# Seven products for the last six input tiles of the second down projection, in a two-layer hybrid model kernel

## The chip, the cores and the metric

The kernel runs on one core of one Trainium2 chip. The metric is the device time of one execution in microseconds (us), as the median of several runs. Before the change it is 2143.97 us, the median of 3 runs that lie between 2143.37 and 2144.52 us.

## What is computed

The reference is a model of two layers on one sequence of T = 1024 tokens with D = 1024 channels, all in float32. Each layer is a mixer followed by a feed-forward block with a short causal convolution, both added to a running sum `h`; a last norm scales the result. The change lies in the feed-forward blocks and in that last norm:

```python
def conv_ffn(hn, w_up, conv_w, conv_b, w_down):
    up = causal_dwconv(hn @ w_up, conv_w) + conv_b
    gate, val = jnp.split(up, 2, axis=-1)
    return (jax.nn.silu(gate) * val) @ w_down
...
        h = h + conv_ffn(rms_norm(h, norm_ffn[layer]), ffn_w_up[layer], ...)
    return rms_norm(h, norm_final)
```

The hidden width is 2816, which is 22 tiles of 128 channels. So the down projection of a layer has 22 input tiles and 8 output tiles.

## The kernel before

Everything is kept with channels on the 128 partitions and tokens along the free axis. `H[0..7]` are the eight channel tiles of the running sum, each 128x1024. A float32 product is made of three TensorE matmuls (`mm3`, L316): each operand is split into a high part and a low part (hi is a rounded copy, lo the difference), and hi·hi, hi·lo and lo·hi are summed in PSUM.

**Seven products.** Most projections are not done tile by tile but two output tiles at a time by a Strassen scheme: the weight block of two output tiles and the token blocks are combined so that seven products stand for eight. `load_pair` (L285) loads four weight pieces and makes seven weight operands from them on ScalarE (ACT) and VectorE (DVE). `pair_product` (L766) runs one product: for each of its `kk` input tiles one `mm3` over 512 columns. There are seven moving operands, o = 0 to 6, of which four are token blocks themselves or a first difference that is stored already split ("whole" ones), and three must be loaded and split again.

**The feed-forward block** (`ffn`, L823). For p = 0 to 21 the up projection of one pair of gate and value tiles runs as seven products; `gate` and `hidden` (L934, L939) do the convolution and the product, and `store_parts` (L863) writes the operands of the down projection to DRAM: whole ones as hi and lo to `p_dram` (L880), others as they are to `s_dram` (L881). All of these DMAs, the two loads that the second half of the tiles needs (L894, L895), the weights (L292) and the operand loads are issued on one queue, SyncE's (SP).

The down projection then runs in sets c of input tiles: sets 0 and 1 have 8 tiles each (two halves of 4, so kk = 4), for t = 0 to 3 pairs of output tiles and o = 0 to 6. While the last pair (t = 3) of a set runs, `load_set` (L908) fills each operand's place for the next set as soon as a product has read it. A whole operand is 8 DMAs of 256 KB (L914) straight into its place. For the others, each piece is first loaded into one of eight half buffers of "room" (L917, L922), that is, `R` and three 128x1024 tiles of the pool `tp`, and then ACT writes hi (L924) and DVE lo (L925) into the place.

The two layers differ. Layer 0 (`third` is true) has a set 2 for the last 6 input tiles, kk = 3, also by seven products. Its operands lie in other places than those of the set before, so that a place freed by product o takes operand (o + 4) % 7: operands 0 to 3 come four products after their place is free, the others eleven. Layer 1 has only sets 0 and 1, with every operand in its own old place, seven products later. Its last 6 input tiles are stored as plain split tiles (L870, two DMAs of 512 KB a tile), loaded by `load_parts`, and multiplied in `final` without the scheme: 8 output tiles x 6 input tiles x `mm3`.

**The end** (`final`, L1036, with `part`, L516). Three stretches of tokens follow one another, of 512, 256 and 256 columns, here called s0, s1 and s2. Each goes through output tiles m = 0 to 7: 18 matmuls, then DVE adds PSUM to `H[m]` (L553), ACT squares it (L407), DVE sums the squares (L411). The weights are loaded and split once (`load_kept`, L276) and kept in the memory `s1`. The norm of s0 goes beside TensorE, through DVE, GpSimd (POOL) and DRAM (`norm_beside`, L424). That of s1 goes through TensorE: `norm_tok` (L456) sums over partitions by matmuls with ones (L480), DVE and POOL make the factor (L470 to L472), and `norm_row` (L482) spreads it by matmuls (L489). `norm_tok` of s1 is put after m = 2 of s2, `norm_row` after m = 4. The scaling of s0 and s1 (`scale`, L1041) is put beside the tiles of s2, every second tile of s0 on POOL (L1047).

**What sets the order.** TensorE's instructions, and those of all other engines, are not run quite as they are written: a planner in the framework puts each engine's instructions in a fixed list by its own estimate of when each is ready, so a load may stand in the queue earlier than the code has it. On the chip each engine and each queue then works through its list in order, and an instruction that waits holds up all behind it.

Of the kernel before, what the change touches and what calls it, by code (L numbers as in the profile page):

```python
# [13 lines left out]
F32 = mybir.dt.float32  # L14
# [89 lines left out]
class Block:  # L104
    def __init__(self, ctx, tc, I, out, stop=None):
# [34 lines left out]
        pad(self.perm, 104, "pad2")  # L140
        self.nhalo = 0
# [45 lines left out]
    def quarter_order(self):  # L187
# [10 lines left out]
        for layer in range(2):  # L198
# [11 lines left out]
            if layer == 0:  # L210
                o += [(("ffn_v0", t), 7) for t in range(4)]
# [611 lines left out]
    def ffn(self, layer, gain):  # L823
        nc, I = self.nc, self.I
        V, A = nc.vector, nc.scalar
        third = gain is not None
        sets = 3 if third else 2
        y_dram = self.tc.dram_tile([NPAIR, P, T], F32, name=f"yf_dram{layer}")
        s_dram = self.tc.dram_tile([sets, 5, 4, P, HALF], F32, name=f"sf_dram{layer}")

        p_dram = self.tc.dram_tile([sets, 4, 4, 2, P, HALF], F32, name=f"pf_dram{layer}")
        if not third:
            l_dram = self.tc.dram_tile([NPAIR - 16, 2, P, T], F32, name=f"lf_dram{layer}")
        depth = lambda c: 4 if c < 2 else 3

        def where(c, o):

            if c == 0 or not third:
                return self.operand(o)
            if c == 1:  # L840
                return self.operand((o + 3) % 7)
            if o < 3:
                i = (20, 14, 26)[o]
                return self.slots1(i, 6).rearrange("p (s n c) -> p n s c", n=2, c=256)
            return self.s2[:, :, 6 * (o - 3):6 * (o - 2), :]
# [15 lines left out]
        room, loads = {}, [0, 0, 0]  # L861

        def store_parts(p, y, hi):  # L863

            hi = hi.bitcast(F32R)
            lo = self.parts.tile([P, T], F32R, tag="lo", name="lo")
            if p >= 16 and not third:
                self.split_half(y, (hi, lo))
                for e, t in enumerate((hi, lo)):
                    nc.sync.dma_start(l_dram[p - 16, e], f32(t))  # L870
                return
# [9 lines left out]
            store = lambda o, r: nc.sync.dma_start(s_dram[c, place[o], k % kk], r)  # L881
# [12 lines left out]
            nc.sync.dma_start(halves(t3), blocks(y_dram[p - kk])[:, :, 1])  # L894
            nc.sync.dma_start(t2, s_dram[c, place[1], k - kk])  # L895
# [9 lines left out]
            else:  # L905
                nc.sync.dma_start(halves(s_dram[c, place[5], k % kk]), v[:, :, 0])

        def load_set(c, o):  # L908
# [7 lines left out]
            if c not in room:  # L916
                ts = [self.R] + [self.t() for _ in range(3)][::-1]  # L917
                room[c] = [t[:, i * HALF:(i + 1) * HALF] for i in range(2) for t in ts]
            for k in range(kk):
                r = room[c][loads[c] % 8]  # L920
                loads[c] += 1
                nc.sync.dma_start(r, s_dram[c, place[o], k])  # L922
                hi, lo = (x[:, :, e + k, :] for e in (0, kk))
                A.copy(hi, halves(r))  # L924
                V.tensor_tensor(lo, halves(r), f32(hi), ALU.subtract)  # L925

        def load_parts(p):
            places = self.place2(p - 16)
            for n in range(2):
                for e in range(2):  # L930
                    nc.sync.dma_start(f32(places[n][e]), l_dram[p - 16, e][:, n * HALF:(n + 1) * HALF])
            return places
# [6 lines left out]
        def hidden(p, tg):  # L939
            tv = conv(NPAIR + p, self.halo[1])  # L940
            V.tensor_tensor(tg, tg, tv, ALU.mult)  # L941
            if (third or p < 16) and p % 8 < depth(p // 8):
# [25 lines left out]
        ys = {}  # L968
        following = {0: {1: (4, 5), **{o: ((o + 4) % 7,) for o in range(2, 7)}},
                     1: {2: (0,), 3: (1, 2), 4: (3,), 5: (4,), 6: (5, 6)}}  # L970
        plain = {0: {1: (0, 1), **{o: (o,) for o in range(2, 7)}}, 1: {}}
        for c in range(sets):
            done = self.down_steps(gain) if c == 2 else {}
            for t in range(4):
                sums, banks = self.pair_added(t), {}
                key = (f"ffn_w{layer}", c, t) if c < 2 else (f"ffn_v{layer}", t)
                for o in range(7):
                    sums(o, self.pair_product(banks, o, self.quarter(key, o), x=where(c, o)))
                    if t == 3 and c < 2:
# [983 lines left out]
```

## Time and profile before

| | us |
|---|---|
| median of 3 runs | 2143.97 |
| the profiled execution's own time | 2145.08 |
| its span, from the first to the last instruction | 2143.2 |
| PE (TensorE matmul) busy | 2127.4 |
| DVE busy | 1722.2 |
| ACT busy | 1077.3 |
| POOL busy | 100.5 |

The profile is of one execution. In its views PE is the matmul side of TensorE and PEld its weight loads; SPq and POOLq are DMA queues; L820 is line 820 of the kernel before. In a table of windows, `(x87)` is the number of recorded instructions that fall into the stretch, PEclk the share of its clock that TensorE was granted, and "DMA share" the mean busy share of the 16 DMA engines. A matmul is shown with its full duration, though the next starts before it ends; its pace is the distance from start to start. A few matmul records are missing.

### The profile page before, as it was taken

To read this page: it belongs to the slowest core of one execution; us is meant where nothing else is said; L and a number is where in the kernel's file an instruction comes from. 1 tells how busy PE (TensorE), PEld (TensorE's weight loads), DVE (VectorE), ACT (ScalarE), POOL (GpSimd) and SP (SyncE) were. 2 spreads that over 40 slices of the span, in tenths; PEclk is the share of its full clock that TensorE was granted. 3 is DMA by queue.
4 is the path that set the end of the run, shared out by engine and by line. 5 is a ranking of instruction groups with operands and counts; after the bars stand their busy time and mean duration, and the time that the engine had idled before them with its cause. 6 is when DMAs were issued, how large, how long until landed. Compare 5 with 4: busy or idle time off the path is not lost.

```text
span 2143.2 us, 29749 instructions
## 1 busy us (share of the span) xinstructions
PE 2127.4 (99%) x10648; PEld 1771.9 (83%) x10648; DVE 1722.2 (80%) x2630; ACT 1077.3 (50%) x1750; POOL 100.5 (5%) x115
## 2 busy tenths in 40 slices
PE   9999999999999999999999999999999999999998
PEld 7878888888888888887888888888888888888887
DVE  7995677776998989988868786768999889878645
ACT  6444423135665555555324576756655555554222
POOL 0102122300000000000000000000000000000002
PEclk9999999999999999999999999999999999999999
DMA  5354433543145435448745212142354445375542
GB/s 188 91 170 126 136 94 94 172 142 118 46 172 178 160 137 179 172 172 289 233 161 172 72 57 80 64 158 65 123 186 163 149 151 177 118 262 183 182 169 85
DMA packets 242021, 313.23 MB, mean 146 GB/s; under 512 B 62432, under 2 KB 129424, under 8 KB 241872
## 3 DMA queue, kind: packets, MB, share of 16 engines
q1 hardware_dynamic: 205632, 304.15, 42.5%
q10 hardware_dynamic: 35088, 6.36, 1.5%
q8 instruction: 84, 1.38, 0.3%
q0 software_dynamic: 1152, 0.81, 0.2%
q14 instruction: 65, 0.53, 0.1%
HBM read 215.79 MB, written 95.45 MB: 145 GB/s over the span
## 4 chain that ended last, share of the span: by engine, by line
PE 63%; issue 30%; DVE 3%; DMA 2%; POOL 1%; SPq 0%; ACT 0%; POOLq 0%; DVEq 0%
PE ps L319 19%; PE ps L320 18%; PE ps L321 18%; PE pc L319 1%; PE pc L321 1%; PE pc L320 1%; DMA s<-pf_dram 1%; DMA t<-sf_dram 0%; DVE wlo L273 0%; DVE l L1416 0%; DVE l L1418 0%; DVE h L1387 0%; PE pc L1551 0%; PE ps L1595 0%; PE pc L1663 0%
## 5 line engine op out<-in xcount | busy, mean ns | idle before, releaser
L319 PE MATMUL ps<-s,whi 128*128 128x512 f32 (+1 forms) x2692 | 1049.1, 391 | 1.5 <-DVE h L820 0.9
L320 PE MATMUL ps<-s,whi 128*128 128x512 f32 (+1 forms) x2692 | 1044.1, 388 | 2.1 <-DVE s L925 1.9
L321 PE MATMUL ps<-s,wlo 128*128 128x512 f32 (+1 forms) x2692 | 1042.7, 388 | 0.6 <-DVE wlo L273 0.6
L272 ACT CAST whi<-raw 128x512 fp32r<-128x512 f32 (+2 forms) x616 | 374.1, 613 | 611.9 <-PE ps L320 471.6
L319 PEld LDWEIGHTS ps<-s,whi 128*128 128x128 f32 x2692 | 505.8, 188 | 107.0 <-ACT whi L272 1.6
L320 PEld LDWEIGHTS ps<-s,whi 128*128 128x128 f32 x2692 | 505.9, 188 | 106.1 <-DVE s L925 4.6
L321 PEld LDWEIGHTS ps<-s,wlo 128*128 128x128 f32 x2692 | 505.6, 188 | 104.5 <-DVE wlo L273 1.4
L273 DVE TENSOR_TENSOR wlo<-raw,whi 128x512 fp32r<-128x512 f32 (+2 forms) x616 | 415.0, 680 | 50.8 <-ACT whi L272 42.3
L852 DVE SCALAR_TENSOR_TENSOR t<-halo,cols,t 128x1024 f32<-128x1024 f32 x176 | 221.6, 1281 | 2.4 <-ACT t L850 1.0
L820 DVE TENSOR_TENSOR h<-ps,h 128x512 f32<-128x512 f32 x140 | 96.3, 689 | 75.7 <-PE ps L321 75.5
L810 DVE TENSOR_TENSOR halo<-ps,kept 128x512 f32<-128x512 f32 (+1 forms) x138 | 91.8, 666 | 71.1 <-PE ps L321 70.5
L850 ACT ACTIVATE t<-halo,cols 128x1024 f32<-128x1024 f32 x88 | 109.5, 1247 | 18.0 <-DVE halo L810 9.0
L805 ACT COPY kept<-ps 128x512 f32<-128x512 f32 (+1 forms) x138 | 77.0, 558 | 11.0 <-PE ps L321 9.6
L472 POOL TENSOR_TENSOR rtok<-rtok,npow 128x4 f32<-128x4 f32 (+1 forms) x10 | 9.9, 990 | 1097.2 <-DVE rtok L471 1097.2
L877 ACT CAST t<-t 128x512 fp32r<-128x512 f32 x68 | 41.2, 621 | 39.1 <-DVE t L941 37.1
L941 DVE TENSOR_TENSOR t<-t 128x1024 f32<-128x1024 f32 x44 | 53.6, 1219 | 0.0
L553 DVE TENSOR_TENSOR h<-ps,h 128x512 f32<-128x512 f32 (+1 forms) x48 | 28.6, 599 | 30.6 <-PE ps L321 30.5
L882 DVE TENSOR_TENSOR t<-t 128x512 f32<-128x512 f32 x76 | 52.1, 686 | 0.6 <-DMA sf_dram<-t 0.6
L936 ACT ACTIVATE t<-t 128x1024 f32<-128x1024 f32 x44 | 46.8, 1063 | 10.4 <-DVE t L852 10.3
L407 ACT ACTIVATE t<-h 128x512 f32<-128x512 f32 (+1 forms) x49 | 26.9, 564 | 45.8 <-DVE h L553 43.8
L878 DVE TENSOR_TENSOR lo<-t 128x512 fp32r<-128x512 f32 x68 | 46.7, 686 | 0.0
L294 DVE TENSOR_TENSOR raw<-raw 128x512 f32<-128x512 f32 (+1 forms) x64 | 43.6, 681 | 3.3 <-issue 1.9
(341 smaller groups left out, 2170.7 us busy)
## 6 DMA issues: line engine op xcount, KB each, us to landing
raw<-in_ffn_up_dram SPq DMA_DIRECT2D x176, 256.0 KB, 2.7
s<-pf_dram SPq DMA_DIRECT2D x136, 256.0 KB, 5.2
sf_dram<-t SPq DMA_DIRECT2D x84, 256.0 KB, 2.4
pf_dram<-t SPq DMA_DIRECT2D x68, 256.0 KB, 2.6
pf_dram<-lo SPq DMA_DIRECT2D x68, 256.0 KB, 2.6
t<-sf_dram SPq DMA_DIRECT2D x67, 256.0 KB, 4.8
raw<-in_ffn_w_dram SPq DMA_DIRECT2D x64, 256.0 KB, 3.1
raw<-in_mix_in_dram SPq DMA_DIRECT2D x52, 256.0 KB, 3.0
```

The lines of the kernel that those rows point to most:

```text
L272: self.nc.scalar.copy(hi[:, 0:w], raw[:, 0:w])
L273: eng.tensor_tensor(lo[:, 0:w], raw[:, 0:w], f32(hi[:, 0:w]), ALU.subtract)
L319: mm(ps, whi, xhi, start=start, stop=False)
L320: mm(ps, whi, xlo, start=False, stop=False)
L321: mm(ps, wlo, xhi, start=False, stop=stop)
L805: A.copy(kept[o], ps)
L810: V.tensor_tensor(dst(i, j), v(ps), v(kept[k]), ALU.add)
L820: V.tensor_tensor(h(*to[o]), ps.rearrange("p (h c) -> p h c", c=256), h(*to[o]), ALU.add)
L850: A.activation(t, buf[:, 2:2 + T], AF.Identity, scale=w(0), bias=self.col(f"ffn_cb{layer}", tile_i))
L852: V.scalar_tensor_tensor(t, buf[:, 2 + j:2 + j + T], w(j), t, ALU.mult, ALU.add)
L882: sub = lambda out, a, b: V.tensor_tensor(halves(out), a, b, ALU.subtract)
L941: V.tensor_tensor(tg, tg, tv, ALU.mult)
```

## The change

1. `store_parts` issues the stores and loads of tiles p = 16 to 21 on POOL's queue, no longer SP's, in both layers. Layer 1 stores these tiles as layer 0 does: per tile 5 DMAs of 256 KB (p = 16 to 18, besides `y_dram` on SP) or 9 (p = 19 to 21, two of them loads).
2. `load_set` has no room any more: a piece that must be split is loaded into the place of its low part, ACT copies hi from there, and DVE takes hi off in place. This holds for both layers. It can start only when the place is free.
3. Layer 1 gets a set 2, and rotates its operands in set 1 as layer 0 does. Its set 2 runs the seven products for t = 0 and 1 only, that is, for output tiles 0 to 3. An eighth operand (o = 7) is loaded during it.
4. `final` computes only m = 4 to 7 by the plain product, from four of the set's operands. The weights of these tiles take 8 places. The squares of `H[0..3]` go over 1024 columns (`final_steps`).
5. The norm of s0 goes through TensorE: `norm_tok` after m = 4 of s1, `norm_row` after m = 5; that of s1 likewise in s2. All tiles of s0 and s1 are scaled on DVE, those of s0 beside m = 6 and 7 of s1 and m = 4 and 5 of s2, those of s1 beside m = 6 and 7 of s2.
6. A spare tile of 40 columns in the pool `sm` takes the 320 bytes of a partition that `norm_beside` no longer needs, so that the operand memory `s2` behind it keeps its address.

```diff
+        pad(self.sm, 40, "pad3")
...
-            if layer == 0:
-                o += [(("ffn_v0", t), 7) for t in range(4)]
+            o += [((f"ffn_v{layer}", t), 7) for t in range(2 if layer else 4)]
...
+            i = ((8, 0, 26, 6, 12, 0, 18, 20) if layer else (20, 14, 26, 0, 6, 12, 18))[o]
+            if o < 3 or o == 7:
                 return self.slots1(i, 6).rearrange("p (s n c) -> p n s c", n=2, c=256)
-            return self.s2[:, :, 6 * (o - 3):6 * (o - 2), :]
+            return self.s2[:, :, i:i + 6, :]
...
+            queue = nc.gpsimd if p >= 16 else nc.sync
...
-            if p >= 16 and not third:
-                self.split_half(y, (hi, lo))
-                for e, t in enumerate((hi, lo)):
-                    nc.sync.dma_start(l_dram[p - 16, e], f32(t))
-                return
...
-                    nc.sync.dma_start(p_dram[c, whole[c][o], k % kk, e], f32(t[:, at]))
-            store = lambda o, r: nc.sync.dma_start(s_dram[c, place[o], k % kk], r)
+                    queue.dma_start(p_dram[c, whole[c][o], k % kk, e], f32(t[:, at]))
+            store = lambda o, r: queue.dma_start(s_dram[c, place[o], k % kk], r)
...
-            if c not in room:
-                ts = [self.R] + [self.t() for _ in range(3)][::-1]
-                room[c] = [t[:, i * HALF:(i + 1) * HALF] for i in range(2) for t in ts]
             for k in range(kk):
-                r = room[c][loads[c] % 8]
-                loads[c] += 1
-                nc.sync.dma_start(r, s_dram[c, place[o], k])
                 hi, lo = (x[:, :, e + k, :] for e in (0, kk))
-                A.copy(hi, halves(r))
-                V.tensor_tensor(lo, halves(r), f32(hi), ALU.subtract)
+                if o < 7:
+                    nc.sync.dma_start(f32(lo), halves(s_dram[c, place[o], k]))
+                else:
+                    nc.sync.dma_start(f32(lo), blocks(y_dram[16 + k])[:, :, 1])
+                A.copy(hi, f32(lo))
+                V.tensor_tensor(lo, f32(lo), f32(hi), ALU.subtract)
...
-                     1: {2: (0,), 3: (1, 2), 4: (3,), 5: (4,), 6: (5, 6)}}
-        plain = {0: {1: (0, 1), **{o: (o,) for o in range(2, 7)}}, 1: {}}
+                     1: {1: (1,), 3: (0, 2), 4: (5,), 5: (3,), 6: (4, 6)} if layer
+                     else {2: (0,), 3: (1, 2), 4: (3,), 5: (4,), 6: (5, 6)}}
+        for c in range(3):
+            done = {}
+            if c == 2:
+                done = self.final_steps() if layer else self.down_steps(gain)
+            for t in range(2 if layer and c == 2 else 4):
...
+    def final_steps(self):
+        V, A = self.nc.vector, self.nc.scalar
+        self.acc, self.sq = self.t(), self.t()
+        def square(m):
+            def f():
+                if m == 0:
+                    A.activation(self.acc, self.H[m], AF.Square)
+                    return
+                A.activation(self.sq, self.H[m], AF.Square)
+                V.tensor_tensor(self.acc, self.acc, self.sq, ALU.add)
+            return f
+        self.squares = square
+        return {(1, 1): [square(0)], (1, 3): [square(1)]}
...
+        kept, places = {}, [6, 14, 16, 18, 0, 2, 4, 26]
+        def part(t0, w, room, left):
...
+            for m in range(4, KT):
+                ps = self.pp(both=True)[:, 0:w]
+                for u in range(2):
+                    if (u, m) not in kept:
+                        kept[u, m] = self.load_kept(self.I[name + "ab"[u]][m], places[len(kept)])
+                    hi, lo = kept[u, m]
+                    for kt in range(4 - 2 * u):
+                        c = slice(kt * P, (kt + 1) * P)
+                        xh, xl = (operand(4 * u + kt, e, n, j) for e in range(2))
+                        self.mm3(ps, hi[:, c], lo[:, c], xh, xl, u == 0 and kt == 0, u == 1 and kt == 1)
+                        self.slot()
+                h = self.H[m][:, sl]
+                V.tensor_tensor(h, ps, h, ALU.add)
+                self.square_step(st, m, h, w)
+                for f in left.get(m, ()):
+                    f()
...
-        s0 = part(0, 512, {})
-        self.norm_beside(s0[0], 0)
-        s1 = part(512, 256, {})
-        late = {k: [lambda k=k: scale(*s0, k, R0, nc.gpsimd if k % 2 else V)] for k in range(KT)}
+        late = lambda s, ks, row: [lambda k=k: scale(*s, k, row()) for k in ks]
+        s0 = part(0, 512, more, {4: [self.squares(2)], 5: [self.squares(3)]})
+        s1 = part(512, 256, self.sq[:, 0:HALF],
+                  {4: [lambda: run(self.norm_tok(s0[0]))], 5: [lambda: run(self.norm_row(s0[0], 0))],
+                   6: late(s0, (0, 1), R0), 7: late(s0, (2, 3), R0)})
...
+        s2 = part(768, 256, self.sq[:, HALF:],
+                  {4: late(s0, (4, 5), R0) + [lambda: run(self.norm_tok(s1[0], 256))],
+                   5: late(s0, (6, 7), R0) + [lambda: run(self.norm_row(s1[0], w=256))],
+                   6: late(s1, range(5), R1), 7: late(s1, range(5, 8), R1)})
```

More of the change, by code (lines that the diff above doesn't have):

```diff
@@ L825, in ffn @@
         V, A = nc.vector, nc.scalar
-        third = gain is not None
-        sets = 3 if third else 2
         y_dram = self.tc.dram_tile([NPAIR, P, T], F32, name=f"yf_dram{layer}")
[L829 to L833, printed above, removed]
+        s_dram = self.tc.dram_tile([3, 5, 4, P, HALF], F32, name=f"sf_dram{layer}")
+        p_dram = self.tc.dram_tile([3, 4, 4, 2, P, HALF], F32, name=f"pf_dram{layer}")
         depth = lambda c: 4 if c < 2 else 3
         def where(c, o):
-            if c == 0 or not third:
+            if c == 0:
                 return self.operand(o)
@@ L893, in store_parts @@
             t4 = t3
-            nc.sync.dma_start(halves(t3), blocks(y_dram[p - kk])[:, :, 1])
-            nc.sync.dma_start(t2, s_dram[c, place[1], k - kk])
+            queue.dma_start(halves(t3), blocks(y_dram[p - kk])[:, :, 1])
+            queue.dma_start(t2, s_dram[c, place[1], k - kk])
             store_split(3, v[:, :, 1], first)
@@ L905, in store_parts @@
             else:
-                nc.sync.dma_start(halves(s_dram[c, place[5], k % kk]), v[:, :, 0])
+                queue.dma_start(halves(s_dram[c, place[5], k % kk]), v[:, :, 0])
         def load_set(c, o):
@@ L941, in hidden @@
             V.tensor_tensor(tg, tg, tv, ALU.mult)
-            if (third or p < 16) and p % 8 < depth(p // 8):
+            if p % 8 < depth(p // 8):
                 nc.sync.dma_start(y_dram[p], tg)
@@ L978, in ffn @@
                     sums(o, self.pair_product(banks, o, self.quarter(key, o), x=where(c, o)))
-                    if t == 3 and c < 2:
-                        for q in (following if third else plain)[c].get(o, ()):
+                    if t == 3:
+                        for q in following[c].get(o, ()):
                             load_set(c + 1, q)
-                    if not third and (c, t) == (1, 3) and o in (1, 2):
-                        for p in range(16, 20) if o == 1 else (20, 21):
-                            ys[p] = load_parts(p)
+                    if layer and (c, t, o) == (2, 0, 1):
+                        load_set(2, 7)
                     for f in done.get((t, o), ()):
@@ L988, in ffn @@
                     hidden(NPAIR - 1, gate(NPAIR - 1))
-        if not third:
-            self.final([ys[p] for p in range(16, NPAIR)], f"ffn_d{layer}")
+        if layer:
+            self.final(f"ffn_d{layer}")
+    def final_steps(self):
[11 more added lines that the diff above has]
+        return {(1, 1): [square(0)], (1, 3): [square(1)]}
     def down_steps(self, gain):
@@ L1034, in xplace, with final @@
         return ((0, 1, 2, 5, 3, 4, 6, 7)[k] * 4 + 2 * e) * HALF
-    def final(self, ys, name):
+    def final(self, name):
         nc = self.nc
         V = nc.vector
+        more = self.t()
         def scale(st, sl, k, pr, eng=V, queue=nc.sync):
```

44 lines of the change are left out of this document (15 added, 29 removed).

## The prediction

> **What bounds the kernel now.** I read the page's table of engines first, then a table of windows cut at the borders of the down projections' sets, then the timeline of TensorE at those borders, and last the waits.
>
> ```profile
> span 2143.2 us, 29749 instructions
> PE 2127.4 (99%) x10648; PEld 1771.9 (83%) x10648; DVE 1722.2 (80%) x2630; ACT 1077.3 (50%) x1750; POOL 100.5 (5%) x115
> ```
>
> TensorE is busy for 99% of the span, so time is won by taking matmuls out or by closing the few places where it starves, and lost by new waits of TensorE. The timeline gives the pace and the price of a norm on TensorE: the first plain matmul of s0, the first two of s1, and, from the end of layer 0, three matmuls around `norm_tok` and three around `norm_row` of a 512-column norm.
>
> ```profile
> 2064.92 0.39 PE L319 MATMUL ps<-s,s 128*128 128x512 f32 x1
> ...
> 2097.56 0.28 PE L319 MATMUL ps<-s,s 128*128 128x256 f32 x1
> 2097.68 0.28 PE L320 MATMUL ps<-s,s 128*128 128x256 f32 x1
> ...
> 1208.09 0.40 PE L321 MATMUL ps<-s,wlo 128*128 128x512 f32 x1
> 1208.42 0.65 PE L480 MATMUL pc<-t,ones 128*32 128x128 f32 x16
> 1208.99 0.50 PE L319 MATMUL ps<-s,whi 128*128 128x512 f32 x1
> ...
> 1209.56 0.40 PE L321 MATMUL ps<-s,wlo 128*128 128x512 f32 x1
> 1209.80 1.05 PE L489 MATMUL pc<-ident,rtok 128*128 128x128 f32 x8
> 1210.60 0.47 PE L319 MATMUL ps<-s,whi 128*128 128x512 f32 x1
> ```
>
> s0 has 8 x 6 x 3 = 144 matmuls between 2064.92 and 2097.56: 32.64 / 144 = 0.2267 us for 512 columns. For 256 columns the distance is 0.12 us. So a set of 336 matmuls takes 76.16 us at this pace, and layer 0's set 2 (252) takes 57.12 us. The windows are, in order: layer 0's set 0, the stretch in it with the gaps, its sets 1 and 2; layer 1's sets 0 and 1, s0, and s1 with s2.
>
> ```profile
> core 0: us, PE busy (x) PEld busy (x) DVE busy (x) ACT busy (x) POOL busy (x), PEclk, DMA share, GB/s
> 985.20:1066.80 81.60, 78.52 (x336) 62.21 (x335) 67.41 (x104) 35.51 (x58) 0.00 (x0) 1.00 0.74 252
> 989.40:1010.00 20.60, 17.52 (x68) 11.67 (x67) 14.06 (x22) 11.59 (x17) 0.00 (x0) 1.00 0.94 343
> 1066.80:1143.20 76.40, 76.40 (x337) 62.84 (x337) 50.59 (x81) 22.31 (x39) 0.00 (x0) 1.00 0.60 204
> 1143.20:1201.40 58.20, 57.28 (x254) 47.14 (x253) 52.29 (x92) 30.31 (x58) 0.00 (x0) 1.00 0.34 111
> 1911.80:1988.80 77.00, 76.84 (x337) 62.48 (x336) 65.04 (x99) 34.54 (x56) 0.00 (x0) 1.00 0.70 236
> 1988.80:2064.90 76.10, 76.10 (x337) 63.05 (x336) 45.95 (x72) 19.26 (x32) 0.00 (x0) 1.00 0.52 179
> 2064.90:2097.60 32.70, 32.70 (x146) 27.07 (x145) 14.80 (x25) 11.12 (x21) 0.00 (x0) 1.00 0.25 85
> 2097.60:2133.30 35.70, 35.70 (x309) 35.27 (x307) 23.58 (x46) 7.97 (x18) 8.95 (x9) 1.00 0.29 98
> ```
>
> The clock is full in all of them. Against the pace, layer 0's set 0 loses 81.60 - 76.16 = 5.44 us, layer 1's 77.00 - 76.16 = 0.84 us; layer 0's set 2 loses 58.20 - 57.12 = 1.08 us; the four others lose next to nothing. In the stretch with the gaps the DMA engines are 0.94 busy. The waits of TensorE there (first two rows) and in layer 0's set 2 (third) name the splits of late operands, late weights and a PSUM bank that is cleared late; the last two rows are SP's own waits while it should be loading.
>
> ```profile
> PE ps L320 <- DVE s L925: 1.7, 5, 0.5
> PE ps L321 <- DVE wlo L273: 0.6, 1, 0.6
> ...
> PE ps L319 <- DVE h L820: 0.9, 1, 0.9
> ...
> SPq L881 <- DVE t L882: 2.1, 1, 2.1
> SPq L894 <- DVE s L925: 3.2, 1, 3.2
> ```
>
> **The closing block: matmuls.** Before, s0 is 144 x 0.2267 = 32.64 us and s1 with s2 288 x 0.12 = 34.56 us, together 67.20. After, set 2 of layer 1 is 2 x 7 x 3 x 3 = 126 matmuls of 512 columns (28.56 us), s0 72 (16.32 us), s1 and s2 144 of 256 columns (17.28 us): 62.16. That takes out 5.04 us. The scheme itself gives 4.08 (18 matmuls of 512 columns fewer); the other 0.96 comes from 144 narrow matmuls that become 72 wide ones, since 2 x 0.12 is more than 0.2267.
>
> The Trainium skill, "TensorE: Matmul & The Clock Gate", section "Back-to-back issue gap", gives a gap of N / 2.4 + 2.5 ns, 0.216 and 0.109 us for these widths, by which an estimate of the saving would be 4.1 us; the rows above are longer, and I keep theirs.
>
> **The norm of s0 on TensorE.** `norm_tok` pushes the next matmul from 0.23 to 1208.99 - 1208.09 = 0.90 us, `norm_row` from 0.23 to 1210.60 - 1209.56 = 1.04: +0.67 + 0.81 = 1.48 us. The norm of s1 is paid before and after. `norm_beside` cost TensorE nothing. Net so far -3.56 us.
>
> **Waits at the end.** From the sums of the last norm to its factor, at the end of the program where nothing hides it:
>
> ```profile
> 2134.42 0.32 PE L480 MATMUL pc<-t,ones 128*32 128x64 f32 x8 [0.72 <-ACT t L407]
> 2136.15 0.71 PE L489 MATMUL pc<-ident,rtok 128*128 128x128 f32 x4 [1.41 <-POOL rtok L472]
> ```
>
> That is 1.73 us. Now one tile (18 x 0.12 = 2.16 us), no longer two, lies between `norm_tok` and `norm_row`, with all matmuls behind `norm_row` on TensorE's list. It just fits, if DVE is free. I take 0.25 us for each of the two norms; the ends are nothing and the whole 1.41 us of the row.
>
> DVE is fuller there, and the price of its work depends on POOL:
>
> ```profile
> 2115.23 0.75 DVE L1044 SCALAR_TENSOR_TENSOR h<-h,cols,R 128x512 f32<-128x512 f32 x1 [1.92 <-DMA R<-nrow_dram]
> ```
>
> ```profile
> L1044 DVE SCALAR_TENSOR_TENSOR h<-h,cols,R 128x512 f32<-128x512 f32 x4 | 5.7, 1436 | 1.9 <-DMA R<-nrow_dram 1.9
> L1044 DVE SCALAR_TENSOR_TENSOR h<-h,cols,pc 128x256 f32<-128x256 f32 x8 | 3.5, 475 | 0.0
> L553 DVE TENSOR_TENSOR h<-ps,h 128x256 f32<-128x256 f32 x16 | 6.5, 418 | 5.8 <-PE ps L321 5.8
> ```
>
> The 512-column scaling takes 0.75 us by the first row and 1.44 in the mean of the four that ran while POOL scaled the other tiles. POOL's half is gone, so 0.75 holds. As written, DVE's work in s2 is 7 x 0.42 (four sums from PSUM, three of squares) + 4 x 0.75 + 8 x 0.475 = 9.7 us, TensorE's 72 x 0.12 + 1.0 = 9.6 us. s1 has 7 x 0.42 + 4 x 0.75 = 5.9 us and room for more. I take 0.3 us for the last sum arriving late; the ends are 0 and 2.8 (4 x 0.69, if the scalings still cost 1.44). The block then gives -3.56 + 0.5 + 0.3 = -2.76 us. The rest of the tail (last factor, last scalings, output DMAs) is unchanged.
>
> **The start of set 0, twice.** The stores and loads of tile p = 20 leave SP's queue. In layer 0 that frees SP of the 2.1 us behind L881, which comes in the middle of the operand loads, and of the block behind L894, after which the weights came 0.6 us late: 5.44 - 2.1 - 0.6 = 2.7. The bytes stay, and the DMA engines are 0.94 busy. In layer 1 the same tile now moves 9 x 256 KB in place of two transfers of 512 KB, five units more. A row of a saturated stretch, around the step from set 0 to set 1 of layer 0, gives the unit:
>
> ```profile
> 1054.00:1086.00 32.00, 32.00 (x142) 26.07 (x141) 19.94 (x33) 10.28 (x17) 0.00 (x0) 1.00 1.02 356
> ```
>
> At 356 GB/s 256 KB take 0.74 us, so layer 1 has 3.7 us more to move here, less the waits that SP is rid of. After the change both layers run the same code here; I take 2.5 us lost in each: 5.0 in place of 6.28, -1.28 us. Ends: 0.2 each (what set 1 of layer 0 loses), -5.9; 5.44 each, +4.6.
>
> The Trainium skill, "Trainium Kernel Development and Optimization", section "Key Constraints", says that DMAs from the SP, ACT and POOL queues share the same 16 engines and interleave, so that another queue saves issue time only. It speaks against this edit; the 0.94 agrees with it, SP's 2.1 us of waiting do not.
>
> **The step from set 0 to set 1, twice.** Without room, pieces to be split can't come ahead of time. Before, in layer 0, the first of set 1's whole operands is issued at 1050.94, and seven pieces for the room went ahead of it:
>
> ```profile
> 1042.51 2.63 SPq L922 DMA_DIRECT2D t<-sf_dram  x3
> ...
> 1046.04 1.38 SPq L922 DMA_DIRECT2D t<-sf_dram  x3
> 1049.84 0.32 SPq L922 DMA_DIRECT2D R<-sf_dram  x1
> 1050.94 1.18 SPq L914 DMA_DIRECT2D s<-pf_dram  x2
> ```
>
> They now fall into the stretch that is already saturated (share 1.02): 7 x 0.74 = 5.2 us more. Against that, operand 4's place is free one product before that of operand 5, so four of them may still run in the idle time ahead, and products 4 to 6 have eleven products' notice, which the planner can use. I take 0.75 us in each layer (layer 1 rotates like layer 0 now): +1.5; ends 0 and 5.2 each.
>
> **The step from set 1 to set 2.** Layer 1 gets it newly; layer 0 loses 1.08 us in it. I take +1.0, ends 0 and 2.2. Layer 0's own I leave as it is (-1.1 to +2). The extra splitting of tiles 16 to 21 in layer 1 is what layer 0 already does beside the up projection; a POOL issue is one instruction on an engine that is 5% busy; the pad costs nothing, since it keeps addresses. The eighth operand and the eight weights have all of set 2 as cover; without it they would cost one landing, a few us.
>
> **The sum.** -2.76 - 1.28 + 1.5 + 1.0 = -1.54 us against the profiled execution's 2145.08 (its span is 2143.2, and 1.9 lie around it): 2143.54. That execution is 1.11 us above the median of the runs, so the forecast is 2142.4 us. About 0.2%, or 4.3 us, is what a measurement of this kernel can tell from no change.
>
> **Rivals.** First, SP's blocked queue was the whole cause at set 0: both layers then lose only 0.2 us, and rotations and set 2 start without loss. -2.76 - 5.88 = -8.64: 2135.3 us. For it: layer 1, with two stores in place of nine DMAs, lost only 0.84. Against it: the DMA share of 0.94. Second, it ends slower because operands that must be split come too late at the step from set 0 to set 1: the full 5.2 us in both layers, -2.76 - 1.28 + 1.0 + 10.4 = +7.4: 2151.3 us. It is slower by over 0.2% once a rotation loses more than 3.7 us. For it: the share of 1.02 and the static lists, on which a late split also holds up DVE's clearing of PSUM. Against it: layer 0's rotation loses only 0.2 now. Third, the page's rule in this kernel's terms: bytes and not the queue set the start of set 0, so both layers lose 5.44 there: -2.76 + 4.6 + 1.5 + 1.0 = +4.3: 2148.3 us. Fourth, the end is eaten up by DVE and the norms at their upper ends (2.8 + 2.8): +2.04 - 1.28 + 2.5 = +3.3: 2147.2 us, no change.
>
> **How the numbers follow.** Forecast 0.40, first rival 0.34, second 0.12, third 0.08, fourth 0.06. Faster: the first and 0.02 of the forecast's spread, 0.36. Slower: the second and half of the third, 0.16. Same: 0.48. The range from 2135 to 2150 takes in the forecast, the first, third and fourth and leaves out the second; the forecast's own is 2139 to 2146.
>
> **What would show it.** Right: 126 + 72 matmuls of 512 columns and 144 of 256 at the same paces; 62 us and two norms of s0 and s1 in the closing block; about 2.5 us of gaps at the start of both sets 0; gaps under 1 us at the steps to set 1, with the DMA share near 1. Wrong: gaps of several us at those steps, with L924 or L925's successors as releaser (second rival), no gaps at set 0 (first), or `norm_row` waiting for POOL by over 1 us in s1 and s2 (fourth); a pace other than 0.2267 or 0.12 us would upset the whole sum.

## The result, and the profile after

The changed kernel takes 2157.97 us (median of 4 runs, 2157.84 to 2159.16) where the kernel before took 2143.67 (4 runs): a ratio of 1.0068, with a 95% interval from 1.005 to 1.0085. I had forecast 2142.4. First the head of the profile page of the changed kernel, whose profiled execution took 2157.84 us:

```profile
span 2155.8 us, 29889 instructions
PE 2130.2 (99%) x10582; PEld 1766.8 (82%) x10582; DVE 1742.0 (81%) x2672; ACT 1083.1 (50%) x1763; POOL 140.1 (6%) x191
```

The span is 12.6 us longer. There are 66 fewer recorded matmuls, yet PE is busy for longer (2130.2 against 2127.4), in part because a matmul at half clock counts as busy, as we shall see. To find the place, take from the timeline the start of the last sum from PSUM (L820) of each set, layer 0's sets 0, 1 and 2 and layer 1's sets 0 and 1:

```profile
1068.13 0.68 DVE L820 TENSOR_TENSOR h<-ps,h 128x512 f32<-128x512 f32 x1
1148.07 0.69 DVE L820 TENSOR_TENSOR h<-ps,h 128x512 f32<-128x512 f32 x1
1206.37 0.68 DVE L820 TENSOR_TENSOR h<-ps,h 128x512 f32<-128x512 f32 x1
1999.41 0.68 DVE L820 TENSOR_TENSOR h<-ps,h 128x512 f32<-128x512 f32 x1
2080.07 0.68 DVE L820 TENSOR_TENSOR h<-ps,h 128x512 f32<-128x512 f32 x1
```

Before, these stood at 1066.82, 1143.87, 1201.58, 1988.96 and 2065.12. So up to the end of layer 0's set 0 the change loses 1.3 us, in its set 1 2.9, in its set 2 0.6, from there to the end of layer 1's set 0 5.7, in layer 1's set 1 4.5; the rest wins 2.35. (DVE's last sum of layer 1's set 1 comes 1.6 us after set 2's first matmul, 0.2 us before the change; so 1.4 of the 4.5 us belong to the rest.)

The waits of the changed kernel between 975 and 1012 us, the start of layer 0's set 0:

```profile
ACT s L913 <- DMA s<-sf_dram: 4.7, 1, 4.7
DVE s L914 <- ACT s L913: 4.3, 2, 4.0
...
DVE t L873 <- DMA sf_dram<-t: 3.1, 1, 3.1
PE ps L319 <- DVE h L820: 3.0, 1, 3.0
...
PE ps L319 <- DVE halo L810: 1.3, 1, 1.3
```

Before, SP waited 2.1 us for DVE and TensorE had five short waits for late splits. Now DVE waits: 3.1 us at L873 until a store of tile 20 on POOL's queue has landed, since the buffer is written anew, and 4 us at L914 for an operand piece that ACT can't split because its load is still under way. What stands behind these on DVE's list is the clearing of PSUM (L810, L820), and TensorE waits for that, 3.0 us in one go. It pays once more behind such a gap, as its timeline shows (start, duration):

```profile
990.91 0.39 PE L321 MATMUL ps<-s,wlo 128*128 128x512 f32 x1
994.29 0.77 PE L319 MATMUL ps<-s,whi 128*128 128x512 f32 x1 [3.00 <-DVE h L820]
...
995.28 0.63 PE L321 MATMUL ps<-s,wlo 128*128 128x512 f32 x1
995.71 0.63 PE L319 MATMUL ps<-s,whi 128*128 128x512 f32 x1
...
997.68 0.39 PE L321 MATMUL ps<-s,wlo 128*128 128x512 f32 x1
```

```profile
985.00:990.00 5.00, 5.00 (x23) 4.13 (x22) 1.44 (x3) 2.44 (x4) 1.28 (x2) 1.00 1.08 388
990.00:996.00 6.00, 3.00 (x10) 2.20 (x9) 6.00 (x9) 4.05 (x7) 0.00 (x0) 0.84 1.08 391
996.00:1002.00 6.00, 6.00 (x24) 4.83 (x24) 6.00 (x9) 5.57 (x9) 0.00 (x0) 0.88 1.09 384
```

Behind the gap one distance is 0.57 us and six are 0.43 in place of 0.2267, and the granted clock falls to 0.84 and 0.88 of full speed in these windows: 1.5 us more. (The window's columns are as in the prediction; the clock is the third number from the right.)

At the end of the program the forecast holds. The timeline around the norms of s0 (first five rows below) and at the last norm:

```profile
2127.60 0.28 PE L321 MATMUL ps<-s,s 128*128 128x256 f32 x1
2127.81 0.64 PE L480 MATMUL pc<-t,ones 128*32 128x128 f32 x16
2128.38 0.39 PE L319 MATMUL ps<-s 128*128 128x256 f32 x1
...
2130.63 1.09 PE L489 MATMUL pc<-ident,rtok 128*128 128x128 f32 x8
2131.48 0.36 PE L319 MATMUL ps<-s 128*128 128x256 f32 x1
...
2146.61 0.32 PE L480 MATMUL pc<-t,ones 128*32 128x64 f32 x8 [0.72 <-ACT t L407]
2148.42 0.71 PE L489 MATMUL pc<-ident,rtok 128*128 128x128 f32 x4 [1.49 <-POOL rtok L472]
```

Neither `norm_tok` (L480) nor `norm_row` (L489) of s0 waits for anything: only the last norm of the program has a releaser.

### The profile page after: what moved, and what is told of

Its sections match the earlier page's. It is cut to its first block, busy times and chain, and to the rows that moved or that the text cites. A ratio compares the mean times of both kernels' runs of the same rounds, so it can differ in the third digit from the quotient of the medians.

```text
span 2155.8 us, 29889 instructions
## 1 busy us (share of the span) xinstructions
PE 2130.2 (99%) x10582; PEld 1766.8 (82%) x10582; DVE 1742.0 (81%) x2672; ACT 1083.1 (50%) x1763; POOL 140.1 (6%) x191
## 4 chain that ended last, share of the span: by engine, by line
PE 89%; issue 4%; DMA 3%; DVE 3%; POOL 1%; ACT 0%; SPq 0%; POOLq 0%; DVEq 0%; ACTq 0%
PE ps L319 27%; PE ps L321 26%; PE ps L320 26%; DMA s<-sf_dram 2%; DMA sf_dram<-t 1%; DMA s<-pf_dram 1%; PE pc L319 1%; PE pc L321 1%; PE pc L320 1%; PE ps L1662 0%; PE ps L1664 0%; PE ps L1663 0%; DVE t L848 0%; PE pc L489 0%; PE pc L1570 0%
## 5 line engine op out<-in xcount | busy, mean ns | idle before, releaser
L319 PE MATMUL ps<-s,whi 128*128 128x512 f32 (+1 forms) x2734 | 1067.1, 392 | 10.5 <-DVE h L820 5.0
L320 PE MATMUL ps<-s,whi 128*128 128x512 f32 (+1 forms) x2734 | 1061.0, 388 | 0.8 <-DVE s L914 0.8
L321 PE MATMUL ps<-s,wlo 128*128 128x512 f32 (+1 forms) x2734 | 1059.3, 388 | 2.4 <-DVE wlo L273 2.4
L319 PEld LDWEIGHTS ps<-s,whi 128*128 128x128 f32 x2734 | 514.3, 188 | 123.2 <-ACT whi L272 4.7
L321 PEld LDWEIGHTS ps<-s,wlo 128*128 128x128 f32 x2734 | 514.1, 188 | 108.6 <-DVE wlo L273 3.7
L320 PEld LDWEIGHTS ps<-s,whi 128*128 128x128 f32 x2734 | 514.7, 188 | 106.0 <-DVE s L914 2.1
L820 DVE TENSOR_TENSOR h<-ps,h 128x512 f32<-128x512 f32 x154 | 105.6, 687 | 73.8 <-PE ps L321 73.2
L810 DVE TENSOR_TENSOR halo<-ps,kept 128x512 f32<-128x512 f32 (+1 forms) x138 | 91.6, 664 | 65.8 <-PE ps L321 65.3
L913 ACT CAST s<-s 128x512 fp32r<-128x512 f32 x77 | 47.3, 620 | 47.4 <-DMA s<-sf_dram 41.1
L914 DVE TENSOR_TENSOR s<-s 128x512 fp32r<-128x512 f32 x77 | 50.4, 686 | 23.2 <-ACT s L913 22.7
L871 POOL DMA_DIRECT2D pf_dram<-t x24 | 13.2, 549 | 830.8 <-ACT t L868 830.3
L873 DVE TENSOR_TENSOR t<-t 128x512 f32<-128x512 f32 x88 | 60.1, 684 | 6.9 <-DMA sf_dram<-t 6.8
L869 DVE TENSOR_TENSOR lo<-t 128x512 fp32r<-128x512 f32 x80 | 54.7, 684 | 0.0
```

Of the source, the lines that this page charges most:

```text
L319: mm(ps, whi, xhi, start=start, stop=False)
L320: mm(ps, whi, xlo, start=False, stop=False)
L321: mm(ps, wlo, xhi, start=False, stop=stop)
L810: V.tensor_tensor(dst(i, j), v(ps), v(kept[k]), ALU.add)
L820: V.tensor_tensor(h(*to[o]), ps.rearrange("p (h c) -> p h c", c=256), h(*to[o]), ALU.add)
L873: sub = lambda out, a, b: V.tensor_tensor(halves(out), a, b, ALU.subtract)
```

## The experiments

All were timed beside the kernel before on the same chip, five rounds each; on those chips it had medians of 2144.2 to 2144.8 us, so ratios are compared, not times. The table gives the profiled span of each and, stage by stage as above, its difference from the kernel before in us. One profile each, so tenths mean little.

| kernel | ratio (95%) | span | L0 to end of set 0 | L0 set 1 | L0 set 2 | to end of L1 set 0 | L1 set 1 | rest |
|---|---|---|---|---|---|---|---|---|
| the change | 1.0068 (1.0050 to 1.0085) | 2155.8 | +1.3 | +2.9 | +0.6 | +5.7 | +4.5 | -2.4 |
| queue undone | 1.0069 (1.0056 to 1.0081) | 2158.7 | +3.0 | +3.5 | +0.1 | +6.1 | +5.1 | -2.3 |
| room back | 1.0026 (1.0016 to 1.0035) | 2147.6 | -0.5 | +0.4 | -0.9 | +6.0 | +1.9 | -2.6 |
| both undone | 1.0013 (1.0004 to 1.0022) | 2146.1 | -0.7 | +0.3 | -0.6 | +4.7 | +1.1 | -1.8 |
| before + queue | 1.0005 (0.9996 to 1.0014) | 2143.5 | +0.6 | 0.0 | -1.0 | +0.5 | 0.0 | +0.2 |
| before + split in place | 1.0039 (1.0027 to 1.0052) | 2149.0 | +0.7 | +2.1 | +0.5 | +2.5 | +0.2 | -0.2 |
| no transfers of tile 20 | 0.9961 (0.9948 to 0.9973) | 2134.4 | -6.5 | +0.1 | -0.7 | -1.1 | +1.3 | -1.9 |
| no arithmetic of tile 20 | 1.0013 (1.0004 to 1.0022) | 2144.6 | 0.0 | +0.1 | -0.7 | +3.7 | +0.9 | -2.6 |
| tile 20 in set 0 | 0.9993 (0.9984 to 1.0001) | 2140.6 | -5.7 | +2.5 | -1.1 | -0.1 | +3.5 | -1.7 |
| tile 20 in set 1 | 0.9965 (0.9952 to 0.9977) | 2134.3 | -6.6 | +0.3 | -0.7 | -0.8 | +0.9 | -2.0 |
| before + tile 20 in set 0 | 0.9991 (0.9982 to 1.0000) | 2141.4 | -4.8 | +2.6 | -0.6 | +0.2 | 0.0 | +0.9 |
| before + tile 20 in set 1 | 0.9972 (0.9961 to 0.9983) | 2136.7 | -6.1 | +0.4 | -1.1 | +0.2 | 0.0 | +0.2 |
| no pad | 1.0163 (1.0150 to 1.0177) | 2175.3 | +9.2 | +3.6 | +1.4 | +13.6 | +4.6 | -0.3 |

**Queue undone.** The changed kernel with one line put back:

```diff
-            queue = nc.gpsimd if p >= 16 else nc.sync
+            queue = nc.sync
```

> The changed kernel, with the stores and loads of tiles 16 to 21 put back on SP's queue; everything else stays changed. In the changed kernel TensorE loses about 7.3 us at the start of layer 0's set 0 and 6.6 at that of layer 1, against 5.4 and 0.8 before. Theory Q (POOL's queue lets tile 20's stores fight with the operand loads, and DVE waits 3.1 us for one of them to land): both layers lose about 5.4 us there, as layer 0 did before, so about 3 us are won: 2155. Theory I (operands that are split in their own place block ACT's and DVE's lists until the load lands): the loss stays or grows, since the loads come later behind SP's waits: 2158 to 2161. The steps from set 0 to set 1 keep their 3.3 us each under both.

No difference in the time: the intervals lie on each other. But the waits have other names. Its waits of TensorE between 975 and 1020 us:

```profile
PE ps L320 <- DVE s L914: 1.8, 4, 0.6
PE ps L319 <- ACT s L913: 1.1, 2, 0.6
PE ps L320 <- DMA s<-pf_dram: 0.2, 1, 0.2
```

These are late operands, many and short, where the changed kernel has few and long waits for PSUM. The clock falls all the same: behind two waits of 0.6 us it is at half from 1000.83 to 1004.25 us, and eight matmuls in a row are 0.43 us apart:

```profile
1000.83:1004.25 3.42, 3.42 (x10) 2.66 (x9) 1.64 (x3) 3.11 (x6) 0.00 (x0) 0.50 1.09 383
```

So the kind of wait doesn't decide whether the clock falls. Theory Q, which wanted 3 us, fails as a cause of the loss; theory I's "stays or grows" fits.

**Room back.** The changed kernel with the room for early loads:

```diff
+            if o < 7 and c not in room:
+                ts = [self.R] + [self.t() for _ in range(3)][::-1]
+                room[c] = [t[:, i * HALF:(i + 1) * HALF] for i in range(2) for t in ts]
...
-                    nc.sync.dma_start(f32(lo), halves(s_dram[c, place[o], k]))
+                    r = room[c][loads[c] % 8]
+                    loads[c] += 1
+                    nc.sync.dma_start(r, s_dram[c, place[o], k])
```

> The changed kernel, with the room back: a piece that must be split is loaded ahead of time into one of eight half buffers and split from there, as in the kernel before; POOL's queue and the new end stay. Theory I: the two steps from set 0 to set 1 lose their 3.3 us each no longer, the step from set 1 to set 2 loses about 1 us, and at the start of set 0 the wait of 3 us for DVE's late clearing of PSUM and the slow clock behind it (1.6 us) go in both layers: 2158 - 6.6 - 1 - 9 = about 2141. Theory Q: the starts of set 0 keep their loss, since the stores still fight with the loads: 2158 - 7.6 = about 2150.

Some 9 us come back (1.0026 against 1.0068). The steps from set 0 to set 1 do as theory I has it. The windows 1040 to 1054 and 1066 to 1078 us, ahead of layer 0's step and in it, of the kernel before, the changed kernel, and this one:

```profile
1040.00:1054.00 14.00, 14.00 (x64) 11.59 (x63) 12.23 (x21) 5.57 (x11) 0.00 (x0) 1.00 0.79 257
...
1066.00:1078.00 12.00, 12.00 (x53) 9.52 (x52) 5.77 (x9) 3.11 (x5) 0.00 (x0) 1.00 1.08 385
```

```profile
1040.00:1054.00 14.00, 14.00 (x63) 11.62 (x62) 9.57 (x15) 4.40 (x8) 0.00 (x0) 1.00 0.34 111
...
1066.00:1078.00 12.00, 11.12 (x46) 7.87 (x45) 6.80 (x12) 2.61 (x5) 0.00 (x0) 1.00 1.09 382
```

```profile
1040.00:1054.00 14.00, 14.00 (x64) 11.59 (x63) 11.17 (x19) 5.96 (x10) 0.00 (x0) 1.00 0.68 228
1066.00:1078.00 12.00, 12.00 (x52) 9.09 (x51) 5.78 (x9) 3.11 (x5) 0.00 (x0) 1.00 1.08 387
```

Without room the DMA engines are 0.34 busy ahead of the step, with it 0.79 and 0.68. In the step they are full in all three (1.08, 1.09): what isn't loaded ahead comes late, and 46 matmuls run in place of 52 or 53. But theory I wanted the starts of set 0 to be cured as well. Layer 1's is not (+6.0), so the room is not its cause.

**Both undone.** Both edits together, that is, the seven products and the new end alone.

> The seven products for output tiles 0 to 3 and the new end alone: room back and the stores on SP's queue. The closing block gives -3.6 us against the kernel before. If the scheme costs nothing else: 2140. If layer 1's start of set 0 becomes like layer 0's, because it has to issue nine transfers for tile 20 (5.4 us lost in place of 0.8) and its step to set 2 costs 1 us as in layer 0: 2143.7 - 3.6 + 4.6 + 1 = about 2145.7. Under theory I it lies close to or above the version with the room back alone, under theory Q below it by about 3 us.

Still slower than the kernel before, by 2.8 us, near the second figure. The end wins its share; layer 1's way to the end of set 0 costs 4.7. With the room, POOL's queue looks worse than SP's (1.0026 against 1.0013, though the intervals overlap). What the profiles show beside that: with POOL's queue there is a wait of 2.2 us in layer 1 with eight distances of 0.43 us behind it (1.7 us in all), with SP's queue only shorter waits and none of this.

**The queue alone.** The kernel before, with `queue` as in the change.

> The kernel before with one part of the change: the stores and loads of tiles 16 to 21 on POOL's queue. As I predicted (SP is rid of its blocked spells, 2.7 us lost at layer 0's set 0): 2141. If SP's blocked queue was the whole cause: 2138.4. Theory Q (stores on POOL's queue fight with the loads, DVE waits for one to land): layer 0's set 0 loses 7 us or more in place of 5.4, layer 1's also more than 0.8: 2146 to 2148.

No measurable difference, neither my 2.7 us won nor 2 to 4 lost. The waits of DVE between 965 and 1000 us and of TensorE between 975 and 1012 tell why the gain failed:

```profile
DVE s L926 <- ACT s L925: 7.3, 3, 4.0
DVE t L883 <- DMA sf_dram<-t: 3.5, 1, 3.5
```

```profile
PE ps L319 <- DVE h L820: 3.4, 2, 2.1
PE ps L319 <- DVE halo L810: 1.8, 1, 1.8
```

SP is rid of its wait, and DVE has it instead: its next difference (L883) overwrites what the store on POOL's queue still reads.

**Tile 20's transfers or its arithmetic.** Two kernels on the base of "both undone". The first leaves out the nine transfers of tile 20 (two copies on DVE stand for its two loads, and set 2 reads another tile's operands in its place), the second its splits and differences (the nine transfers stay, but SP no longer waits for ACT and DVE between them):

```diff
-                for e, t in enumerate((hi, lo)):
+                for e, t in enumerate((hi, lo) if p != 20 else ()):
...
-            store = lambda o, r: queue.dma_start(s_dram[c, place[o], k % kk], r)
+            store = lambda o, r: queue.dma_start(s_dram[c, place[o], k % kk], r) if p != 20 else None
```

```diff
-                A.copy(halves(hi[:, at]), src)
-                V.tensor_tensor(halves(lo[:, at]), src, f32(halves(hi[:, at])), ALU.subtract)
+                if p != 20:
+                    A.copy(halves(hi[:, at]), src)
+                    V.tensor_tensor(halves(lo[:, at]), src, f32(halves(hi[:, at])), ALU.subtract)
```

> The seven products and the new end alone, with the nine transfers of tile 20 left out in both layers (the loads of its operands read another tile's in their place, and two copies on DVE stand for the two loads); its arithmetic on ACT and DVE stays. If the bytes of these transfers are the cause: about 2147.2 - 9 = 2138, as little lost as when the tile's stores come later, or less. If ACT's and DVE's work on the tile beside the splits of the weights and operands is the cause: 2147.

> The seven products and the new end alone, with tile 20's arithmetic left out in both layers (no splits, no differences; what is stored is the tile itself or what was loaded); its nine transfers stay on SP's queue. If the bytes are the cause: 2147, though SP no longer waits for ACT and DVE between them, which gives up to 2 us a layer if those waits cost anything. If the arithmetic is: about 2138.

Without the transfers 11 us go (0.9961 against 1.0013), and both starts are free of waits. Without the arithmetic nothing goes. The start of set 0 in layer 1, with both undone, without transfers, and without arithmetic. The windows have the same place in the kernel: without transfers the last clearing of the up projection (L810) starts at 1904.34 us in place of 1908.42 and 1908.34, so its window lies 4 us earlier.

```profile
1900.00:1930.00 30.00, 28.08 (x116) 21.00 (x115) 19.95 (x33) 12.54 (x21) 0.00 (x0) 1.00 1.00 354
```

```profile
1896.00:1926.00 30.00, 30.00 (x134) 24.83 (x133) 27.24 (x44) 17.07 (x27) 0.00 (x0) 1.00 0.92 325
```

```profile
1900.00:1930.00 30.00, 28.46 (x120) 21.88 (x119) 18.19 (x29) 13.31 (x22) 0.00 (x0) 1.00 1.04 366
```

With the transfers the DMA engines are full (1.00, 1.04), whatever DVE does (33 or 29 instructions); without them the share is 0.92, and TensorE gets in all 134 matmuls. The engines are nearly as busy, but with one tile less ahead of the set's operands. That settles the start of set 0: it is the nine transfers, and since issuing them elsewhere changed no time, it is their bytes on the DMA engines and not their place on SP's queue.

**Tile 20 later.** The bytes can stand elsewhere, since set 2 is the only reader. Beside the up projection the tile is stored as it is (512 KB), and its operands are made later, at first while t = 1 of set 0 runs:

```diff
-            if p % 8 < depth(p // 8):
+            if p % 8 < depth(p // 8) or p == 20:
                 nc.sync.dma_start(y_dram[p], tg)
-            store_parts(p, tg, tv)
+            if p != 20:
+                store_parts(p, tg, tv)
...
+                if (c, t) == (0, 1):
+                    y = self.t()
+                    nc.sync.dma_start(y, y_dram[20])
+                    store_parts(20, y, self.t())
```

> The seven products and the new end alone (room back, stores on SP's queue), and tile 20's operand stores taken out of the start of set 0: beside the up projection the tile is only stored as it is (512 KB, one transfer), read back while t = 1 of set 0 runs, and its nine transfers and splits follow there. Without this step the version measured 2147.2 us against 2144.4 before, with 5.0 us lost at the start of layer 0's set 0 and 5.6 at that of layer 1. If the bytes and the work of tile 20 in the stretch where the operands must come in are the cause (theory B): seven units of 0.65 us, the distance of SP's issues there, go in both layers, so about 4.5 us each: 2138. If the start is limited by the set's own operands, whatever stands beside them (theory S), nothing comes back: 2147.

> The kernel before, with tile 20's operand stores taken out of the start of set 0 in the same way, in layer 0 alone (layer 1 of that kernel has two transfers for the tile). Theory B: layer 0's set 0 loses about 1 us in place of 5.5, as layer 1's does before: 2140. Theory S: 2144.4.

The starts of set 0 are cured as expected, in this version and in the kernel before. But beside "both undone" 2.2 and 2.4 us are given back in the steps to set 1 (2.6 in the kernel before), about half of the gain, which neither theory had. So the next version moves it once more, to `(c, t) == (1, 1)`:

> As the version that stores tile 20's operands while t = 1 of set 0 runs, but now while t = 1 of set 1 runs, where nothing else is loaded; set 2 needs them only at its own start. The version with t = 1 of set 0 measured 2142.6 us against 2144.8 before and loses nothing at the starts of set 0, but 2.7 and 3.3 us at the steps from set 0 to set 1, where 0.5 and 0.3 were lost without the deferral. If the late transfers of tiles 20 and 21 push those of the room's pieces into the step (theory B, bytes and their place): these 5.2 us come back, 2137.5. If the steps lose because operands now start earlier in another way, with no link to where tile 20 lies: 2142.6.

Measured 0.9965 (2136.43 us beside 2144.18): 7.7 us faster than the kernel before, and some 22 faster than the change (by the ratios). The step from set 0 to set 1, 1054 to 1078 us, with the tile in set 0 and in set 1:

```profile
1054.00:1066.00 12.00, 12.00 (x53) 9.58 (x52) 8.31 (x14) 3.95 (x7) 0.00 (x0) 1.00 1.08 384
1066.00:1078.00 12.00, 11.01 (x47) 8.13 (x46) 4.51 (x7) 3.04 (x5) 0.00 (x0) 1.00 1.08 391
```

```profile
1054.00:1066.00 12.00, 12.00 (x55) 9.94 (x54) 5.93 (x10) 3.54 (x6) 0.00 (x0) 1.00 1.08 385
1066.00:1078.00 12.00, 12.00 (x52) 9.29 (x51) 6.07 (x10) 2.41 (x5) 0.00 (x0) 1.00 1.07 394
```

Both are saturated. What differs lies ahead: the first early load into a `t` buffer of the room, in set 0 and in set 1:

```profile
1042.24 0.37 SPq L920 DMA_DIRECT2D t<-sf_dram  x1
```

```profile
1033.87 0.38 SPq L920 DMA_DIRECT2D t<-sf_dram  x1
```

With tile 20 in set 0, SP issues stores of the two tiles 20 and 21 until 1042 us, ahead of these loads on its list, and the loads begin 8 us later: between 1030 and 1036 us the DMA share is 0.14, against 0.70. The same deferral in the kernel before, in layer 0 alone, sorts the gain:

> The kernel before with tile 20's operands of layer 0 stored while t = 1 of set 1 runs, and nothing else changed: how much of the 7.7 us of the best version so far (2136.4 against 2144.2) is the seven products and the new end, and how much the moved transfers of layer 0 alone. By the rows, layer 0's set 0 loses about 0 in place of 5.5 us and its set 2 0.5 less: 2138.5 on a level of 2144.2, so that the seven products and the end leave 2 us, which is their 3.6 less the 1.8 us that layer 1's step to set 2 loses. If the step from set 0 to set 1 takes part of it back as it did with the stores in set 0: 2141 to 2142.

Measured 0.9972 (2138.49 us), as expected. Six of the 7.7 us are the moved transfers of layer 0; the seven products and the new end leave 1.7. The two intervals overlap, so by the runs alone these can't be told from no gain; the stages put them at about 2 us.

**Split in place, alone.** The kernel before without room, pieces loaded into the place of their low part:

```diff
-                r = room[c][loads[c] % 8]
-                loads[c] += 1
-                nc.sync.dma_start(r, s_dram[c, place[o], k])
                 hi, lo = (x[:, :, e + k, :] for e in (0, kk))
-                A.copy(hi, halves(r))
-                V.tensor_tensor(lo, halves(r), f32(hi), ALU.subtract)
+                nc.sync.dma_start(f32(lo), halves(s_dram[c, place[o], k]))
+                A.copy(hi, f32(lo))
+                V.tensor_tensor(lo, f32(lo), f32(hi), ALU.subtract)
```

> The kernel before with one part of the change: no room, pieces that must be split are loaded into the place of their low part and split there, in both layers. As I predicted (0.75 us a step from set 0 to set 1): about 2146. From the pair of the changed kernel and the changed kernel with the room back, which lie 8 to 9 us apart: 3.3 us at each step from set 0 to set 1 and 2 to 3 us at the start of layer 0's set 0: 2153 to 2154. If layer 1's own order of operands, in which each place is refilled by the same operand seven products later, leaves enough time there: 2150.

1.0039: 7.5 us slower, so this edit alone costs more than the 0.2% that can be told, in either kernel. The last case of the expectation is nearest: layer 1's set 1 loses nothing in the order of that kernel, where a place is refilled seven products ahead. But 2.5 us are lost up to the end of layer 1's set 0, which no case had and no run here takes apart.

**No pad.** The changed kernel without `pad(self.sm, 40, "pad3")`.

> The changed kernel without the spare 40 columns that keep the operand memory at its address; nothing else is changed. If the address matters for the transfers or the matmuls' reads, the paces of 0.2267 and 0.12 us or the time of a 256 KB load would change: 144 matmuls of 512 columns more by one hundredth each are 0.3 us, and over the whole kernel up to 20 us. If it doesn't: 2158.5, the changed kernel's time on this chip's level, within 2 us.

20 us slower than the change (1.0163 against 1.0068). The timeline in layer 0's set 1, nine matmuls in a row, with the pad and without (a line number is one lower there):

```profile
1106.13 0.39 PE L319 MATMUL ps<-s,whi 128*128 128x512 f32 x1
...
1107.95 0.39 PE L321 MATMUL ps<-s,wlo 128*128 128x512 f32 x1
```

```profile
1114.79 0.39 PE L318 MATMUL ps<-s,whi 128*128 128x512 f32 x1
...
1116.66 0.39 PE L320 MATMUL ps<-s,wlo 128*128 128x512 f32 x1
```

Eight distances are 1.82 us with the pad and 1.87 without: 0.2275 and 0.2338 us, though the duration shown is 0.39 in both. The slow distances go by products. Without the pad, the last 36 of each 84 matmuls in this set are 0.231 to 0.234 us apart (from 1109.19, 1128.49 and 1147.79 us on), and in layer 0's set 2 the last 36 of each 63 (from 1192.24 and 1206.78 on); but for about three at the border, the others stay at 0.226 to 0.228. By the kernel's `where` and `operand` these are the matmuls that read their operand from `s2`: three products of 12, and four of 9. Over the whole run the distances between 0.23 and 0.245 us have 23.0 us above 0.2267 in them, in the change 3.4. The difference of 19.6 us is the whole of the 19.5 us by which the span is longer. Which address would do is open, since only this one shift was run.

## Why the prediction was wrong

By its own terms, in us (the measured ones from the profiles of before and after; 1.4 is moved from layer 1's set 1 to the rest, as said above, which leaves -0.95 there. Layer 1's set 2 takes from 2078.46 to the first matmul of s0 at 2109.24, 30.8 us for 126 matmuls in place of 28.56: 2.2 us of step, and so -3.15 for the block):

| term | forecast | measured |
|---|---|---|
| closing block | -2.76 | -3.15 |
| starts of set 0, both layers | -1.28 | +7.0 |
| steps from set 0 to set 1, both | +1.5 | +6.0 |
| step to set 2 in layer 1 | +1.0 | +2.2 |
| layer 0's set 2 | 0 | +0.6 |
| sum | -1.54 | +12.65 |

**The closing block** was right, in mechanism and size. The paces stay; `norm_tok` and `norm_row` of s0 push the next matmuls by 0.66 and 0.85 us (2128.38 - 2127.60 - 0.12, and 2131.48 - 2130.51 - 0.12, where the matmul ahead of the latter starts at 2130.51), and the one behind each by 0.1 more, 1.69 in place of 1.48. The 0.5 us for waits did not come. From the start of the last matmul to the end it is 10.4 us in place of 10.0, near the 0.3 that I had put for DVE. That makes -5.04 + 1.69 + 0.4 = -2.95, which agrees with the -3.15 of the stages.

**The starts of set 0** are where it failed, on two counts. That it "frees SP of the 2.1 us behind L881" was true and worth nothing: the queue alone changes no time. A wait for the tile's data moved from SP's list to DVE's, and the bytes stayed. The third rival, the page's rule that another queue saves issue time only (the Trainium skill, "Trainium Kernel Development and Optimization", section "Key Constraints"), had this right, and I gave it 0.08; the ratios 1.0005, and 1.0069 beside 1.0068, agree with it. And in layer 1 the extra bytes had their price in my own text, 3.7 us, but I set it off against SP's freedom and took 2.5 us lost in place of 0.84. The loss is 4.7 with the queue undone and the room back, 5.7 in the change. It is the third rival's size; the transfers are shown as the cause by leaving them out and by moving them.

**The steps from set 0 to set 1** failed in size. I gave the bound, seven pieces of 0.74 us pushed into a saturated stretch, 5.2 us, and then took 0.75 because the planner could use the idle time ahead. The row ahead of the step shows 0.34 in place of 0.79: it could not, since the places are not yet free. In the changed kernel SP waits there, between 1035 and 1080 us, for products to end before it can load into their places (L910 is such a load):

```profile
SPq L910 <- PE ps L320: 4.2, 1, 4.2
```

Measured are 2.9 and 3.1 us, near the middle of my ends; the second rival's direction was right, at 0.12.

**The step to set 2 in layer 1** came out at the upper end (2.2). Layer 0's set 2 was within its range.

**The pad** I had put at nothing, because it keeps addresses. That holds for the change; what it prevents is dearer than everything else in this case, 20 us.

## What to carry to other kernels

Where the DMA engines are full for a stretch, count the bytes that must cross in it and ask who reads them last: in this kernel, moving a tile's transfers to a time with idle engines was worth 6 us in layer 0, moving them to another queue nothing, and moving them just ahead of the next full stretch gave half of the gain back. Buffers that let loads run early are worth what they bring forward out of a full stretch, so price their removal by that and don't count on a planner. When a change to a pool shifts a matmul's operand, look at the distance between its matmuls, not at their durations.

## What the runs showed of the hardware

A wait of TensorE of 3.0 us in one piece was followed by seven slow distances, mostly of 0.43 us, and waits of 1.95 us (the change) and 2.2 us (room back) in layer 1 by eight or more: 1.5 to 1.7 us each. So were two waits of 0.6 us and the shorter ones about them with the queue undone. One of 2.1 us in layer 0 of "room back" was not, nor was this one without the pad, the longest of all:

```profile
1001.49 0.47 PE L318 MATMUL ps<-s,whi 128*128 128x512 f32 x1 [3.16 <-DVE h L819]
```

So the length of a wait doesn't decide. What fits all 14 profiles is this. The clock is at half for 3.41 us each time (994.07 to 997.48 and 1915.67 to 1919.08 us in the change), and two such starts in one profile lie a whole number of 3.413 us apart (921.60 us are 270 of them). Cut a profile into stretches of that length, with the fall of the clock at the end of the program as the mark where there is no other, and add up in each what the distances between matmuls have above 0.2267 us. The four stretches ahead of a half clock have 2.93 and 2.22 us (the change), 2.44 (room back) and 2.14 (queue undone); no other stretch before the end of the program has more than 1.99. The 3.16 us without the pad fall into two stretches, of 1.69 and 1.81. So the price of a wait hangs on where it falls, too. This is a reading of the profiles; no run here tests it. The Trainium skill, "TensorE: Matmul & The Clock Gate", section "Part 1: The HAM clock gate", tells of half clock after an idle window of about 3.4 us; the length agrees, but the stretches here were idle for 2.1 to 2.9 us of it, not for all. The granted clock of 0.84 and 0.88 in the windows above agrees with the halving: 0.16 and 0.12 of 6 us are together 1.7 us, half of 3.4.

An operand memory that starts 320 bytes off made the distances of the 512-column matmuls that read from it 0.231 to 0.234 us in place of 0.2267, over two in five of them in layer 0's set 1.
